# Logits of the first 128 tokens over the first 128 keys alone, in the attention of block 2

## The chip, the core and the metric

The kernel runs on one core of one Trainium2 chip. The core has a matrix engine (TensorE, PE in the profile; its weight loads have a row of their own, PEld), a vector engine (DVE), an activation engine (ACT), a general engine (POOL) and DMA queues, of which SP issues the large loads here. Each engine works through its own list of instructions in order, and semaphores tie the lists together. The metric is the device time of one execution in microseconds (us), lower is better.

## What is computed

The reference chains two transformer blocks on 256 tokens of width 1024. Block 1 (two layers) and its feed-forward are not touched. Block 2 has two layers, each with three kinds of attention over the same 256 tokens, all with heads of 64 channels and all causal:

```python
# moba_attention, 256 tokens are one block: plain causal attention, 6 heads
s_own = jnp.where(kpos_own[None, :] <= t_pos[:, None], s_own, -jnp.inf)
# dsa_attention: 4 index heads rank the keys, the best 64 stay, then 6 heads over one shared key head
idx_score = jnp.where(key_pos[None, :] <= t_pos[:, None], idx_score, -jnp.inf)
_, sel = lax.top_k(idx_score, n_keep)
# dilated_mixture: 3 groups (dilation 1, 4, 16) x 4 slots, a band of keys at or before the token
ok = (dist >= 0) & (dist <= steps) & (blk * C_BLOCK + ki >= C_BLOCK)
```

A token of the first 128 (the first tile, t = 0) can look at keys 0 to 127 at most; a token of the second tile (t = 1) at all 256.

## The kernel before

**Numbers.** Every large product is made of parts in the type fp32r, which TensorE multiplies in one pass: a value is split in a high part and a rest (`whi` and `wlo` for weights, L210 and L211), and `mm3` (L332, its matmuls at L334 to L336) adds three products. Products in plain f32, such as L575 in block 1, the sums over partitions at L355 and the weighing of values at L1003, show two matmul records each in the trace; an fp32r product shows one.

**Logits.** `to_qt` (L430) stacks the high and the low half of one head's queries over the 128 partitions and transposes them (L441), to a tile `qt2` of 128 x 128 for each head and each tile of 128 tokens. `to_kt` (L446) does so for keys (transposes at L458) and writes two planes of 128 x 256 for each head, low over high and high over low. `scores` (L979) then needs two matmuls for one head and one tile of tokens: the query tile is the stationary operand, loaded anew for each, and a plane of 256 keys streams through it, L980 for the first plane and L981 for the second. The result is half of a PSUM bank, `S[:, t * 256:t * 256 + 256]`.

**Who calls it.** In each layer `layer2` (L1119) makes the index logits (L1146, 4 heads and two tiles of tokens), 6 heads with the mask of the selected keys and 6 with the causal mask (`head2`, L1019), and 4 slots of 3 groups (`slot2`, L1032). That is 4 + 12 + 12 = 28 logits of each tile of tokens. Two layers and two matmuls for each make 112 matmuls for the first tile and 112 for the second, 224 in all.

**Who reads it.** `masked_min` (L983, the DVE instruction at L985) adds the mask, scales, and takes the minimum; for t = 0 it reads columns 0 to 127 alone, as does `index_mask` (`S4[h][:, :n]` at L1064). The columns 128 to 255 that the matmuls of the first tile write are read by nobody. Behind it come the exponential (L1010), the scaling (L1013), transposes of the weights (L995, L997), their copy out of PSUM (L999) and the products with the values (L1003).

**Order.** A planner orders each engine's list when the program is built, by priorities (`cur_priority`, the ranks at L274) and by its own estimates of how long instructions take; nothing in the code fixes where between the projections (L334 to L336) a matmul of `scores` lands. PSUM has two banks with the tag `sc` in this part (`att2_banks`, L264).

Of the kernel before, what the change touches and what calls it, by code (L numbers as in the profile page):

```python
# [18 lines left out]
P = 128  # L19
# [223 lines left out]
def ranked(key):  # L243

    def wrap(f):
        def g(self, *a, **k):
            off = self.rank[key]
            self.tc.cur_priority -= off
            r = f(self, *a, **k)
            self.tc.cur_priority += off  # L250
            return r
        return g
    return wrap


class Build:
# [719 lines left out]
        kt = [self.ap.tile([P, 3, 2, 256], F32R, tag="kt2", name="kt2", bufs=self.kt_bufs) for _ in range(0, n, 3)]  # L976
        return [kt[h // 3][:, h % 3] for h in range(n)], kt

    def scores(self, out, q, kt):  # L979
        self.nc.tensor.matmul(out, q, kt[:, 0, :], start=True, stop=False)  # L980
        self.nc.tensor.matmul(out, q, kt[:, 1, :], start=False, stop=True)  # L981

    def masked_min(self, out, S, mask, nm):  # L983

# [33 lines left out]
    @ranked("hd2")  # L1018
    def head2(self, q, kt, masks):  # L1019

        nc = self.nc
        S = self.bank("sc")
        for t in range(2):
            self.scores(S[:, t * 256:t * 256 + 256], q[t], kt)
        p = self.ap.tile([P, 1152], F32, tag="p3", name="p2", bufs=self.p3_bufs)[:, :384]
        nm = self.stat("nm")
        self.masked_min(p[:, :P], S[:, :P], masks[0], nm[:, 0:1])
        self.masked_min(p[:, P:], S[:, 256:512], masks[1], nm[:, 1:2])
        self.softmax2(nm, (p[:, :P], p[:, P:]))
        return p[:, :P], p[:, P:]  # L1030

    def slot2(self, qs, kts):  # L1032

        nc = self.nc
        p = self.ap.tile([P, 1152], F32, tag="p3", name="p3", bufs=self.p3_bufs)
        p0 = p[:, :384].rearrange("p (g k) -> p g k", g=3)
        p1 = p[:, 384:].rearrange("p (g k) -> p g k", g=3)
        nm, n2 = self.stat("nm"), self.stat("n2")
        for t in range(2):
            S = self.bank("sc")  # L1040
            for g in range(2):
                self.scores(S[:, g * 256:g * 256 + 256], qs[g][t], kts[g])
            v = S.rearrange("p (g k) -> p g k", g=2)
            if t == 0:
                self.masked_min(p0[:, 0:2], v[:, :, :P], self.m0[:, 0:2], nm[:, 0:1])
            else:
                self.masked_min(p1[:, 0:2], v, self.m1[:, 0:2], nm[:, 1:2])
        S = self.bank("sc")
        for t in range(2):
            self.scores(S[:, t * 256:t * 256 + 256], qs[2][t], kts[2])  # L1050
        self.masked_min(p0[:, 2], S[:, :P], self.m0[:, 2], n2[:, 0:1])
        self.masked_min(p1[:, 2], S[:, 256:], self.m1[:, 2], n2[:, 1:2])
        nc.vector.tensor_tensor(nm, nm, n2, op=ALU.min)
        self.softmax2(nm, (p[:, :384], p[:, 384:]))
        return [(p0[:, g], p1[:, g]) for g in range(3)]
# [63 lines left out]
    def layer2(self, l, u, rr, rb):  # L1119

        nc, d = self.nc, self.d
        y = [self.half(k, l) for k in range(KT)]
        o_t = lambda: self.ap.tile([P, 256], F32, tag="o2", name="o2", bufs=3)

        ch = self.chunk2(l, 0)
        qi, iws, vb = [], [], []
        kib, ktb = self.new_kt(2)
        for t, ps in enumerate(self.proj_t(ch, u)):
            raw = self.evac2(ps, 452, rr, t)
            vb.append(self.values_of(ps, 384, 1, rr, t))  # L1130
            iw = self.sp.tile([P, 4], F32, tag="iw", name="iw", bufs=2)
            nc.vector.tensor_scalar(iw, raw[:, 448:452], 0.0625, None, op0=ALU.mult)
            iws.append(iw)
            q = self.rope(raw[:, :384], self.rc2[:, t], self.rs2[:, t], 6, "ri")
            dst = self.new_qt()
            self.to_qt(q[:, :256], 4, dst)
            qi.append(dst)
            self.to_kt(q[:, 256:384], 2, ktb, t)
        qb = self.queries(l, 1, u, rr)
        sel = []  # L1140
        for t in range(2):
            S4 = []
            for h in range(0, 4, 2):
                S = self.bank("sc")
                for j in range(2):
                    self.scores(S[:, j * 256:j * 256 + 256], qi[t][:, h + j, :], kib[0])  # L1146
                    S4.append(S[:, j * 256:j * 256 + 256])
            sel.append(self.index_mask(S4, iws[t], t))
        ob = []
        for pr in range(3):  # L1150
            ps = [self.head2([qb[t][:, h, :] for t in range(2)], kib[1], sel) for h in (2 * pr, 2 * pr + 1)]
            pv = self.bank("pv")
            self.weigh(pv, ps, [[vb[t][:, 0, :] for t in range(2)]] * 2, True, True)
            ob.append(o_t())
            nc.scalar.copy(ob[-1], pv[:, :256])

        ka, qa, va = self.keys(l, 2, u, rr), self.queries(l, 3, u, rr), self.values(l, 4, u, rr)
        gates = self.branch_gates(l, 11, u, rb)
        for i in range(3):
            self.gated(ob[i], gates[i], y[3 + i])  # L1160
        cm = (self.m0[:, 0], self.mcausal)
        oa = []
        for pr in range(3):
            hs = (2 * pr, 2 * pr + 1)
            ps = [self.head2([qa[t][:, h, :] for t in range(2)], ka[h], cm) for h in hs]
            pv = self.bank("pv")
            self.weigh(pv, ps, [[va[t][:, h, :] for t in range(2)] for h in hs], True, True)
            oa.append(o_t())
            nc.scalar.copy(oa[-1], pv[:, :256])

        for pr in range(2):
            kc, qc, vc = self.keys(l, 5 + 3 * pr, u, rr), self.queries(l, 6 + 3 * pr, u, rr), self.values(l, 7 + 3 * pr, u, rr)
            if pr == 0:
                gates += self.branch_gates(l, 12, u, rb)
                for i in range(3):
                    self.gated(oa[i], gates[3 + i], y[i])
            ps = [self.slot2([[qc[t][:, 2 * g + i, :] for t in range(2)] for g in range(3)], [kc[2 * g + i] for g in range(3)])
                  for i in range(2)]
            oc = self.bank("pv")
            for g in range(3):  # L1180
                self.weigh(oc, [ps[i][g] for i in range(2)], [[vc[t][:, 2 * g + i, :] for t in range(2)] for i in range(2)],
                           g == 0, g == 2)
            self.gated(oc[:, :256], gates[6 + pr], y[6 + pr])
        return y
# [103 lines left out]
```

## Time and profile before

| | us |
|---|---|
| median of 3 runs | 1556.16 (1555.87 to 1558.52) |
| the profiled execution | 1556.1 |
| its span, first to last instruction | 1554.3 |
| PE busy in the span | 1499.0 |
| DVE busy | 1004.0 |
| ACT busy | 799.3 |
| block 2, attention of layer 1, about 996 to 1180 us | 184 |
| block 2, attention of layer 2, about 1282 to 1465 us | 183 |

How to read it: all rows come from one profiled execution, so sums are made against its 1556.1 us, 1.8 us of which lie outside the span. Matmuls are pipelined, and the length of one record holds its latency too. What a matmul takes from its neighbours is the distance from its start to the start of the next one, called its slot in this document.

### The profile page before, as it was taken

The numbers are of one execution on the slowest core, as the hardware profiler recorded it, in microseconds if no ns is written. First come the engines' busy times: TensorE is split into PE (matmuls) and PEld (weight loads), VectorE is DVE, ScalarE is ACT, GpSimd is POOL, SyncE is SP. The second block draws the span as 40 slices with busy tenths as digits, with TensorE's granted clock in tenths as the row PEclk, the third lists the DMA queues.
The fourth block names the chain that finished last, engine by engine and source line by source line (L and its number), as shares of the span: only waits on it lengthen the run. The fifth ranks groups of instructions, "written<-read, shape, count | busy, mean of one in ns | idle before, by whom it ended". The sixth has DMA issues, their size and how long they took to land.

```text
span 1554.3 us, 25048 instructions
## 1 busy us (share of the span) xinstructions
PE 1499.0 (96%) x9826; PEld 1290.8 (83%) x9826; DVE 1004.0 (65%) x2210; ACT 799.3 (51%) x1498; POOL 70.4 (5%) x83
## 2 busy tenths in 40 slices
PE   5999999999999999999799999999999999999996
PEld 2875688887788789856599999888899999899996
DVE  5675687333333236867565557898767779987675
ACT  3476665321322224567453436677665556876542
POOL 0300000000000000010000000102100010200000
PEclk9999999999999999999999999999999999999998
DMA  9313355333332524362845554434434544334450
GB/s 375 118 55 147 137 193 184 142 109 136 136 109 81 191 80 160 112 221 101 330 148 186 190 182 152 155 124 161 149 132 167 184 146 153 136 114 157 164 188 30
DMA packets 36982, 238.36 MB, mean 153 GB/s; under 512 B 4224, under 2 KB 5888, under 8 KB 15104
## 3 DMA queue, kind: packets, MB, share of 16 engines
q1 hardware_dynamic: 36576, 236.14, 42.8%
q8 instruction: 77, 1.26, 0.3%
q0 software_dynamic: 288, 0.62, 0.2%
q14 instruction: 41, 0.34, 0.1%
HBM read 236.32 MB, written 1.05 MB: 153 GB/s over the span
## 4 chain that ended last, share of the span: by engine, by line
PE 83%; DVE 10%; ACT 3%; DMA 2%; issue 2%; POOL 0%; SPq 0%; DVEq 0%; ACTq 0%; POOLq 0%
PE mm L334 11%; PE mm L335 11%; PE mm L336 11%; PE g L336 6%; PE g L335 6%; PE g L334 6%; PE dn L335 5%; PE dn L336 5%; PE dn L334 5%; DVE wlo L211 3%; PE mm L492 2%; PE tr L635 2%; PE pv L643 2%; DMA raw<-in_w_ada_dram 1%; PE pv L1003 1%
## 5 line engine op out<-in xcount | busy, mean ns | idle before, releaser
L210 ACT CAST whi<-raw 128x1024 fp32r<-128x1024 f32 (+4 forms) x392 | 370.0, 949 | 496.1 <-PE mm L335 137.4
L211 DVE TENSOR_TENSOR wlo<-raw,whi 128x1024 fp32r<-128x1024 f32 (+4 forms) x392 | 431.3, 1105 | 198.1 <-ACT whi L210 196.2
L335 PE MATMUL dn<-Hl,whi 128*128 128x256 f32 (+1 forms) x520 | 161.7, 311 | 0.0
L336 PE MATMUL dn<-Hh,wlo 128*128 128x256 f32 (+1 forms) x520 | 161.0, 310 | 0.4 <-DVE wlo L211 0.4
L334 PE MATMUL dn<-Hh,whi 128*128 128x256 f32 (+1 forms) x520 | 160.6, 310 | 0.0
L334 PE MATMUL mm<-Hh,whi 128*128 128x256 f32 (+1 forms) x512 | 149.3, 292 | 1.0 <-DVE mod L506 0.7
L336 PE MATMUL mm<-Hh,wlo 128*128 128x256 f32 (+1 forms) x512 | 149.9, 293 | 0.0
L335 PE MATMUL mm<-Hl,whi 128*128 128x256 f32 (+1 forms) x512 | 149.3, 292 | 0.0
L334 PE MATMUL mm<-whi,Hh 128*128 128x384 f32 (+2 forms) x352 | 129.1, 367 | 0.0
L336 PE MATMUL mm<-whi,Hl 128*128 128x384 f32 (+2 forms) x352 | 127.3, 362 | 0.0
L335 PE MATMUL mm<-wlo,Hh 128*128 128x384 f32 (+2 forms) x352 | 127.2, 361 | 0.0
L334 PE MATMUL mm<-Fh,whi 128*128 128x256 f32 (+1 forms) x368 | 123.0, 334 | 1.6 <-ACT Fh L539 1.5
L336 PE MATMUL g<-Fh,wlo 128*128 128x256 f32 (+1 forms) x368 | 123.2, 335 | 0.3 <-DVE wlo L211 0.3
L334 PE MATMUL g<-Fh,whi 128*128 128x256 f32 (+1 forms) x368 | 122.6, 333 | 0.0
L335 PE MATMUL g<-Fl,whi 128*128 128x256 f32 (+1 forms) x368 | 122.6, 333 | 0.0
L335 PE MATMUL mm<-Fl,whi 128*128 128x256 f32 (+1 forms) x368 | 122.2, 332 | 0.0
L336 PE MATMUL mm<-Fh,wlo 128*128 128x256 f32 (+1 forms) x368 | 122.1, 332 | 0.0
L335 PEld LDWEIGHTS dn<-Hl,whi 128*128 128x128 f32 x520 | 99.1, 191 | 8.3 <-issue 2.5
L336 PEld LDWEIGHTS dn<-Hh,wlo 128*128 128x128 f32 x520 | 99.1, 191 | 6.3 <-issue 0.8
L334 PEld LDWEIGHTS dn<-Hh,whi 128*128 128x128 f32 x520 | 99.0, 191 | 5.6 <-ACT whi L210 0.5
L334 PEld LDWEIGHTS mm<-Hh,whi 128*128 128x128 f32 x512 | 97.8, 191 | 2.2 <-ACT whi L210 0.8
L336 PEld LDWEIGHTS mm<-Hh,wlo 128*128 128x128 f32 x512 | 97.8, 191 | 1.6 <-issue 0.8
(283 smaller groups left out, 3240.8 us busy)
## 6 DMA issues: line engine op xcount, KB each, us to landing
raw<-in_w_ada_dram SPq DMA_DIRECT2D x48, 1024.0 KB, 4.9
raw<-in_w_gu_dram SPq DMA_DIRECT2D x44, 1024.0 KB, 4.8
raw<-in_w_mix_dram SPq DMA_DIRECT2D x32, 1024.0 KB, 4.8
raw<-in_w_in_dram SPq DMA_DIRECT2D x40, 768.0 KB, 4.3
raw<-in_w_in_dram SPq DMA_DIRECT2D x20, 1024.0 KB, 4.8
raw<-in_w_dn_dram SPq DMA_DIRECT2D x16, 1024.0 KB, 4.8
raw<-in_w_dn_dram SPq DMA_DIRECT2D x12, 768.0 KB, 4.4
raw<-in_w_out_dram SPq DMA_DIRECT2D x8, 1024.0 KB, 4.9
```

The lines of the kernel that those rows point to most:

```text
L210: self.made.append(nc.scalar.copy(hi[:, :m], x))
L211: self.made.append(nc.vector.tensor_tensor(lo[:, :m], x, hi[:, :m].bitcast(F32), op=ALU.subtract))
L334: self.link(nc.tensor.matmul(out, lhs[0], rhs[0], start=start, stop=False))
L335: self.link(nc.tensor.matmul(out, lhs[0], rhs[1], start=False, stop=False))
L336: self.link(nc.tensor.matmul(out, lhs[1], rhs[0], start=False, stop=stop))
L492: made.append(self.nc.tensor.matmul(ps[32 * g:32 * g + 32, :], self.s32[:, 4 * i + g, :], raws[i][:, 512 * g:512 * g + 512], start=i == fi ...
L635: nc.tensor.transpose(ps[:, (2 * j + qt) * P:(2 * j + qt + 1) * P], p[i][:, qt, c:c + P], self.ident)
L643: first(nc.tensor.matmul(pv[i * 64:i * 64 + 64, :256], v, pts[i][0][:, j * 256:j * 256 + 256], start=b == 0 and j == 0, stop=b == nk // 2 ...
L1003: f(nc.tensor.matmul(pv[64 * i:64 * i + 64, c], vs[i][j], pt[:, d], start=first and j == 0, stop=last and j == 1))
```

## The change

`scores` takes a number of columns, and its callers give 128 for the first tile of tokens and 256 for the second. No instruction is added or taken away; 112 of the 224 matmuls stream 128 columns of keys in place of 256 and write 128 columns of PSUM. The stationary operands and their loads stay. No wait is added.

```diff
-    def scores(self, out, q, kt):
-        self.nc.tensor.matmul(out, q, kt[:, 0, :], start=True, stop=False)
-        self.nc.tensor.matmul(out, q, kt[:, 1, :], start=False, stop=True)
+    def scores(self, out, q, kt, n):
+
+        self.nc.tensor.matmul(out, q, kt[:, 0, :n], start=True, stop=False)
+        self.nc.tensor.matmul(out, q, kt[:, 1, :n], start=False, stop=True)
...
         for t in range(2):
-            self.scores(S[:, t * 256:t * 256 + 256], q[t], kt)
+            n = P * (t + 1)
+            self.scores(S[:, t * 256:t * 256 + n], q[t], kt, n)
...
             for g in range(2):
-                self.scores(S[:, g * 256:g * 256 + 256], qs[g][t], kts[g])
+                n = P * (t + 1)
+                self.scores(S[:, g * 256:g * 256 + n], qs[g][t], kts[g], n)
...
         for t in range(2):
-            self.scores(S[:, t * 256:t * 256 + 256], qs[2][t], kts[2])
+            n = P * (t + 1)
+            self.scores(S[:, t * 256:t * 256 + n], qs[2][t], kts[2], n)
...
                 for j in range(2):
-                    self.scores(S[:, j * 256:j * 256 + 256], qi[t][:, h + j, :], kib[0])
+                    n = P * (t + 1)
+                    self.scores(S[:, j * 256:j * 256 + n], qi[t][:, h + j, :], kib[0], n)
```

## Rows read from the trace of the kernel before

**Rows 1.** The page: busy time of each engine, and the granted clock in 40 slices.

```profile
PE 1499.0 (96%) x9826; PEld 1290.8 (83%) x9826; DVE 1004.0 (65%) x2210; ACT 799.3 (51%) x1498; POOL 70.4 (5%) x83
PEclk9999999999999999999999999999999999999998
```

**Rows 2.** Busy time by stretch: block 2's attention of layers 1 and 2.

```profile
core 0: us, PE busy (x) PEld busy (x) DVE busy (x) ACT busy (x) POOL busy (x), PEclk, DMA share, GB/s
996.00:1180.00 184.00, 179.70 (x1294) 166.90 (x1293) 152.62 (x364) 128.03 (x263) 17.02 (x13) 1.00 0.41 142
1282.00:1465.00 183.00, 179.44 (x1292) 166.83 (x1292) 151.74 (x363) 126.11 (x260) 16.23 (x12) 1.00 0.41 143
```

**Rows 3.** Waits by releaser in 996 to 1180 us: PE's longest; DVE's for logits.

```profile
engine line waited for: us in total, times, longest us
PE tq L458 <- DVE ks L452: 1.4, 2, 1.0
PE tq L458 <- DVE kt L463: 1.0, 1, 1.0
PE tr L995 <- DVE p L1013: 0.6, 1, 0.6
...
DVE p L985 <- PE sc L981: 4.3, 9, 0.9
```

**Rows 4.** Lines L980 and L981: durations in ns (min/median/max), first and last start.

```profile
L980 PEld LDWEIGHTS sc<-kt,qt x112: 186/188/192, 997.8 to 1433.6; 128*128 128x128 f32 x112
L980 PE MATMUL sc<-kt,qt x112: 277/282/387, 998.0 to 1433.7; 128*128 128x256 f32 x112
L981 PE MATMUL sc<-kt,qt x112: 277/282/371, 999.6 to 1433.8; 128*128 128x256 f32 x112
```

**Rows 5.** Timeline, a run of logits: start us, length us, engine, line.

```profile
1102.07 0.28 PE L981 MATMUL sc<-kt,qt 128*128 128x256 f32 x1
1102.07 0.19 PEld L980 LDWEIGHTS sc<-kt,qt 128*128 128x128 f32 x1
1102.19 0.28 PE L980 MATMUL sc<-kt,qt 128*128 128x256 f32 x1
...
1102.77 0.28 PE L981 MATMUL sc<-kt,qt 128*128 128x256 f32 x1
```

**Rows 6.** Timeline, projections of 384 columns, nine in a row, first and last.

```profile
1068.20 0.34 PE L336 MATMUL mm<-whi,Hl 128*128 128x384 f32 x1
...
1069.60 0.34 PE L335 MATMUL mm<-wlo,Hh 128*128 128x384 f32 x1
```

**Rows 7.** Timeline, sums over partitions: four matmuls that stream one column.

```profile
1258.69 0.52 PEld L355 LDWEIGHTS tr<-ones,acc 128*128 128x128 f32 x4 [0.31 <-PE mm L336]
1258.72 0.58 PE L355 MATMUL tr<-ones,acc 128*128 128x1 f32 x4
```

**Rows 8.** Timeline, a logits matmul behind a transpose of 128 columns.

```profile
1099.63 0.22 PE L441 MATMUL tq<-ident_r,qs 128*128 128x128 f32 x1
1099.63 0.19 PEld L980 LDWEIGHTS sc<-kt,qt 128*128 128x128 f32 x1
1099.69 0.33 PE L980 MATMUL sc<-kt,qt 128*128 128x256 f32 x1
1099.76 0.14 PEld L441 LDWEIGHTS tq<-ident_r,qs 128*128 128x128 f32 x1
```

**Rows 9.** Transposes of 128 columns in fp32r: a run of four, and line L441.

```profile
1000.41 0.46 PE L441 MATMUL tq<-ident_r,qs 128*128 128x128 f32 x4
...
L441 PEld LDWEIGHTS tq<-ident_r,qs x184: 137/140/146, 90.9 to 1430.8; 128*128 128x128 f32 x184
L441 PE MATMUL tq<-ident_r,qs x184: 221/247/306, 90.9 to 1430.9; 128*128 128x128 f32 x184
```

**Rows 10.** Products in plain f32 in block 1: a run of four records, and line L575.

```profile
702.62 1.88 PE L575 MATMUL sc<-c,raw 128*128 128x512 f32 x4
...
L575 PE MATMUL sc<-c,raw x24: 592/592/697, 67.0 to 703.9; 128*128 128x512 f32 x24
```

**Rows 11.** DVE's reads of the logits, by shape.

```profile
L985 DVE CUSTOM_DVE_ANT_0 p<-sc,mk x56: 269/419/692, 1067.0 to 1434.5; 128x256 f32<-128x256 f32 x28, 128x128 f32<-128x128 f32 x20, 128x512 f32<-128x512 f32 x8
L985 DVE CUSTOM_DVE_ANT_0 p<-sc,sel x24: 268/347/421, 1016.4 to 1328.8; 128x128 f32<-128x128 f32 x12, 128x256 f32<-128x256 f32 x12
```

## The prediction

> **What bounds the kernel now.** I read the page first. PE is busy for 1499.0 of 1554.3 us, no other engine for more than two thirds, and the granted clock stands at its upper level, 2.4 GHz, in nearly every slice [rows 1]. A busy share is a poor witness for matmuls, since the records overlap, so I then asked for the busy time by stretch in the two places that the change touches. In the attention of block 2, PE is without any matmul for 184.00 - 179.70 = 4.30 us in layer 1 and for 183.00 - 179.44 = 3.56 us in layer 2, at a granted clock of 1.00; DVE is next with about 152 us [rows 2]. The waits say what the few idle microseconds are: transposes that wait for DVE, 1.0 us at the most each [rows 3]. So PE issues one matmul behind the other here, in order, and these stages last as long as the sum of its slots. What one slot gains or loses goes to the end nearly whole. What other engines wait for the logits (4.3 us of DVE in layer 1 [rows 3]) is off that path.
>
> The question is therefore only what the slot of a logits matmul is now and what sets it. The record's length, 282 ns [rows 4], does not tell, since it holds the latency. The timeline does: from 1102.07 to 1102.77 there are six slots, so one is 0.70 / 6 = 0.117 us, and the weight load of the next matmul starts at the start of the present one [rows 5].
>
> **What the change does, part by part.** It takes 128 of 256 streamed columns from 112 matmuls: 28 logits of the first tile in a layer, two matmuls each, two layers, which is half of the 224 in the trace [rows 4]. It adds no instruction, no wait and no DMA. The readers are not touched: DVE reads 128 columns where the tokens are those of the first tile already (20 and 12 of its instructions [rows 11]), so neither DVE nor ACT gets less to do. A logit lands at best half a slot earlier, and DVE's wait for it is off the path; I cost that at nothing, covered by PE's own list.
>
> What is left is the slot of an fp32r matmul of 128 columns that loads its own 128 x 128 weights. The trace has no such matmul, so I bound it by the nearest rows.
>
> First, by columns. Eight slots of 384 columns take 1069.60 - 1068.20 = 1.40 us, 0.175 us each [rows 6]. Against 0.117 us for 256, that is 0.058 us for 128 columns, or 0.455 ns a column, with nothing left over as a fixed cost. If columns alone set the slot, the short one takes 0.058 us and the change saves 0.117 - 0.058 = 0.059 us on each, 112 x 0.059 = 6.6 us.
>
> Second, by weight loads. The sums over partitions load weights of 128 x 128 and stream one column. Four of them have records of 0.25 us that end 0.58 us after the first start, so a slot is (0.58 - 0.25) / 3 = 0.11 us with next to nothing to stream; their loads, of 0.19 us, start (0.52 - 0.19) / 3 = 0.11 us apart [rows 7]. Their loads are as long as those of the logits (188 ns [rows 4]), though their type is plain f32. An fp32r case agrees: behind a transpose of 128 columns, the load of a logits matmul starts at 1099.63, and the matmul's record ends at 1099.69 + 0.33 = 1100.02, which with its usual 0.28 means that it streamed from 1099.74. The short transpose did not give its slot to the next matmul: that one came 0.11 us after its load began [rows 8]. So one load takes 0.11 us of the loading path, one load is under way at a time, and a matmul of 256 columns (0.117 us) just covers it. With 128 columns the load is no longer covered, and the slot falls to 0.11 and not to 0.058 us.
>
> Third, upwards. Plain f32 products go slower: four records of 512 columns and 0.592 us end 1.88 us after the first start, (1.88 - 0.592) / 3 = 0.43 us each, 0.84 ns a column, and each product has two such records [rows 10]. At that rate a product of 128 columns would take 2 x 128 x 0.84 ns = 0.215 us.
>
> The ends are thus 0.058 and 0.215 us. I take 0.11, for the rows that share both the load's length and the short stream [rows 7, 8] are nearest. The sum: 112 x (0.117 - 0.110) = 0.8 us, all of it on PE's path. 1556.1 - 0.8 = 1555.3 us for the profiled execution. The median of the runs is 1556.16, 0.1 above the profiled time, so I say 1555.4. About 0.2% (3.1 us) is what a measurement of this kernel can tell from no change, so this is no change.
>
> **The rivals.** A, slower: short fp32r products lose their rate. All fp32r products in the trace that aren't transposes stream 256 columns or more, so no row shows that the single-pass rate of 0.455 ns a column holds below that. If it falls to that of plain f32, each of the 112 slots grows from 0.117 to 0.215 us, and 112 x 0.098 = 11.0 us go to PE's list, of which the idle of 7.9 us in both stages absorbs little, since PE waits there for DVE at other places [rows 3]. That gives 1567.1 us. It decides from a slot of 0.117 + 3.1 / 112 = 0.145 us on. For it: there is no counterexample. Against it: one pass of plain f32 at 128 columns is 0.107 us and would still hide behind the load; only two passes hurt, and an fp32r product shows one record. 22%.
>
> B, faster: the load overlaps better than I think. Fp32r transposes of 128 columns with weights of 128 x 128 do follow each other at (0.46 - 0.22) / 3 = 0.08 us [rows 9]. At that slot the change saves 112 x 0.037 = 4.1 us, 1552.0 us; if columns alone count, 6.6 us, 1549.5 us. Against it: the loads of transposes are shorter, 140 ns against 188 [rows 4, 9]. The Trainium skill ("TensorE: Matmul & The Clock Gate", section "Back-to-back issue gap") gives about 81 ns for 128 columns in a sustained stream, and N/2.4 + 2.5 ns for a gap with no load in it; estimates by these two figures are 1552.1 and 1549.3 us, and this rival would win. The same page (section "LDWEIGHTS") puts a load of 128 columns at P/1.2, 107 ns, and there the trace agrees, with 0.11 us. 8%.
>
> C, the order: the planner places PE's list by estimates that know of the columns, so matmuls of both layers may change places. A group of transposes that comes up before its operand is a new wait of up to 1.0 us, of which layer 1 has two now [rows 3]; four more give 1559.4 us. Fewer of them can give back a part of the 7.9 us idle [rows 2]: half of it, 1551.4 us. 12% for a loss over 3.1 us, 8% for such a gain.
>
> That the change doesn't do what it says (the untouched half of a bank read by somebody) I exclude: the readers' shapes are listed above.
>
> **How the numbers follow.** The forecast has 50%, A 22%, C 12% down and 8% up, B 8%. So faster 0.16, same 0.50, slower 0.34. The likeliest time is 1555.4 us; its own range, with small shifts of the order, is 1553.0 to 1559.0. The range over 8 in 10 has to take in A, as it holds more than 2 in 10 with the outer part of C; with both bounds of the slot it is 1549.5 to 1567.5.
>
> **What would show it.** In the profile of the changed kernel, the two lines of `scores` (L981 and L982 there) should list 56 matmuls of 128 columns and 56 of 256 each, with loads of 188 ns as before. In a run of short logits the starts should be 0.11 us apart (0.06 to 0.08 for B, 0.2 for A), with load and matmul starting in step. PE's busy time is no measure of it: records get shorter by some 0.05 us while slots stay. The two attention stretches should last 184 and 183 us within half a microsecond. New lines in PE's waits, or another sequence of projections and logits, would speak for C. I am wrong if the slot of a short logit is above 0.145 or below 0.089 us, or if stages move by microseconds while slots do not.

## The result, and the profile after

The changed kernel takes 1564.94 us in the median (1564.08 to 1565.91) against 1556.01 us before: a ratio of 1.0051, with a 95% interval from 1.0038 to 1.0063. It is slower by 8.9 us, and the forecast was no change.

The first reading is the one that the prediction asked for, the two lines of `scores` (durations in ns as min/median/max), and the page's busy times.

```profile
PE 1505.1 (96%) x9826; PEld 1291.5 (83%) x9826; DVE 1004.4 (64%) x2210; ACT 799.5 (51%) x1498; POOL 72.3 (5%) x83
...
L981 PEld LDWEIGHTS sc<-kt,qt x112: 186/188/192, 994.7 to 1443.9; 128*128 128x128 f32 x112
L981 PE MATMUL sc<-kt,qt x112: 221/280/387, 994.7 to 1443.9; 128*128 128x128 f32 x56, 128*128 128x256 f32 x56
L982 PE MATMUL sc<-kt,qt x112: 221/278/327, 996.6 to 1444.1; 128*128 128x128 f32 x56, 128*128 128x256 f32 x56
```

The change is there: 56 short and 56 long matmuls on each line, with loads as long as before [rows 4]. The number of instructions on each engine is that of before [rows 1]. Next, a run of short logits in the changed kernel, loads and matmuls in order of time:

```profile
1106.26 0.22 PE L981 MATMUL sc<-kt,qt 128*128 128x128 f32 x1
1106.26 0.19 PEld L982 LDWEIGHTS sc<-kt,qt 128*128 128x128 f32 x1
1106.31 0.28 PE L982 MATMUL sc<-kt,qt 128*128 128x128 f32 x1
1106.37 0.19 PEld L981 LDWEIGHTS sc<-kt,qt 128*128 128x128 f32 x1
1106.43 0.27 PE L981 MATMUL sc<-kt,qt 128*128 128x128 f32 x1
1106.48 0.19 PEld L982 LDWEIGHTS sc<-kt,qt 128*128 128x128 f32 x1
```

The loads start at 1106.26, 1106.37 and 1106.48, 0.11 us apart, where those of 256 columns start 0.117 us apart [rows 5]. A short matmul is not slower than a long one, and hardly faster. So the 8.9 us are somewhere else. Where they are, two marks show: the copy of the row scales at the start of each layer of block 2 (`rr`), and the last scaling of the output (`fin`). First the kernel before, then the changed one; the last two numbers are the first and the last start in us.

```profile
L938 DVE COPY rr<-r x1: 169/169/169, 980.1 to 980.1; 128x2 f32<-128x2 f32 x1
L938 DVE COPY rr<-rr x1: 169/169/169, 1262.4 to 1262.4; 128x2 f32<-128x2 f32 x1
L1258 DVE SCALAR_TENSOR_TENSOR fin<-xs,vec,tr x8: 475/475/480, 1546.2 to 1548.9; 128x256 f32<-128x256 f32 x8
```

```profile
L938 DVE COPY rr<-r x1: 168/168/168, 982.5 to 982.5; 128x2 f32<-128x2 f32 x1
L938 DVE COPY rr<-rr x1: 169/169/169, 1269.2 to 1269.2; 128x2 f32<-128x2 f32 x1
L1263 DVE SCALAR_TENSOR_TENSOR fin<-xs,vec,tr x8: 472/472/479, 1557.3 to 1560.0; 128x256 f32<-128x256 f32 x8
```

From mark to mark, layer 1 of block 2 takes 1262.4 - 980.1 = 282.3 us before and 1269.2 - 982.5 = 286.7 after; layer 2, to the last `fin`, 286.5 before and 290.8 after. That is 4.4 and 4.3 us more. From the first `rr` to the last `fin`, called block 2's own time from here on, it is 568.8 us before and 577.5 after. Block 1, which the change does not touch, moves the first mark about between 980 and 986 us from one profiled execution to the next (2.4 us between these two), so block 2's own time is the sharper measure, and each experiment below is given with it.

Busy time by stretch, from mark to mark of layer 1 (columns as in [rows 2]), the kernel before first:

```profile
980.10:1262.40 282.30, 276.89 (x2048) 262.09 (x2046) 227.42 (x498) 179.98 (x347) 21.23 (x16) 1.00 0.43 150
```

```profile
982.50:1269.20 286.70, 278.56 (x2048) 261.91 (x2046) 227.24 (x499) 180.09 (x347) 23.64 (x16) 1.00 0.43 148
```

With the same 2048 matmuls and the same granted clock, PE is without a matmul for 5.41 us before and for 8.14 after. What it waits for stands in the waits of the matmuls, over block 2 (us in total, times, longest). The kernel before:

```profile
PE tq L458 <- DVE ks L452: 3.6, 6, 1.0
PE tr L367 <- DVE rf L348: 2.5, 1, 2.5
PE tq L441 <- DVE qs L436: 1.7, 3, 0.9
PE tr L355 <- DVE acc L386: 1.5, 1, 1.5
PE tq L458 <- DVE kt L463: 1.3, 2, 1.0
PE tr L995 <- DVE p L1013: 1.2, 2, 0.6
PE sc L980 <- ACT ir L1064: 0.8, 2, 0.4
```

The changed kernel, without the lines that stayed within 0.2 us (`ks`, `rf`, `acc`, `kt` of the transposes) and without two new ones of 0.2 us:

```profile
PE tr L996 <- DVE p L1014: 2.5, 6, 0.7
...
PE tq L441 <- DVE qs L436: 2.3, 4, 0.9
...
PE sc L981 <- ACT ir L1068: 1.5, 2, 0.7
PE sc L981 <- DVE n L986: 1.0, 4, 0.3
PE pv L1004 <- ACT pt L1000: 0.8, 4, 0.2
PE sc L982 <- DVE kt L463: 0.7, 1, 0.7
```

Over all lines the waits come to 12.6 us in 17 places before and to 18.2 us in 33 after. None of the new ones is longer than 0.7 us; there are more of them, at logits, at transposes of the weights and at the products with the values. One of them close up, with the DVE instructions that PE waits for:

```profile
995.15 0.95 DVE L211 TENSOR_TENSOR wlo<-raw,whi 128x768 fp32r<-128x768 f32 x1
...
995.58 0.33 PE L336 MATMUL mm<-whi,Hl 128*128 128x384 f32 x1
996.13 0.42 DVE L463 CAST kt<-tq 64x256 fp32r<-64x256 f32 x1
...
996.60 0.33 PE L982 MATMUL sc<-kt,qt 128*128 128x128 f32 x1 [0.68 <-DVE kt L463]
```

In the new order four projections stand in PE's list between the first plane's logits of the index heads and the second plane's. That plane is finished by a copy on DVE, which stands behind a split of weights of 0.95 us. In the old order the first index logits began at 998.0 us [rows 4], eight projections stood behind them, and the second plane's came at 999.6 us [rows 4] with no such wait. PE works its list in order, so the projections behind that matmul wait too. The planner wrote a different list: in the two traces, leaving aside the width of the logits, 232 of PE's 9826 records stand at another place in the sequence, 96 of DVE's 2210 and 74 of ACT's 1498.

### The profile page after: what moved, and what is told of

It is laid out like the page before. It is cut to its first block, busy times and chain, and to the rows that moved or that the text cites. A ratio compares the mean times of both kernels' runs of the same rounds, so it can differ in the third digit from the quotient of the medians.

```text
span 1564.1 us, 25036 instructions
## 1 busy us (share of the span) xinstructions
PE 1505.1 (96%) x9826; PEld 1291.5 (83%) x9826; DVE 1004.4 (64%) x2210; ACT 799.5 (51%) x1498; POOL 72.3 (5%) x83
## 4 chain that ended last, share of the span: by engine, by line
PE 83%; DVE 10%; ACT 4%; DMA 2%; issue 2%; POOL 0%; SPq 0%; DVEq 0%; ACTq 0%; POOLq 0%
PE mm L334 11%; PE mm L335 10%; PE mm L336 10%; PE g L335 6%; PE g L336 6%; PE g L334 6%; PE dn L335 5%; PE dn L336 5%; PE dn L334 5%; DVE wlo L211 3%; PE mm L492 2%; PE tr L635 2%; PE pv L643 2%; DMA raw<-in_w_ada_dram 1%; PE pv L1004 1%
```

## The experiments

The ratios below are against runs of the kernel before taken beside each experiment (medians of 1558.05 to 1558.23 us), not against the 1556.01 us above.

Two changes are in one here: what a matmul does on the chip, and what the planner makes of it. To part them, a step after planning replaces the access patterns of chosen matmuls and leaves every list, wait and semaphore as it is:

```python
def stream(nc, names, n, w):          # after the planner has placed everything
    ...
                    t = [[1, n]] if n <= w else [[0, n // w], [1, w]]
                    blk.instructions[k] = copy.replace(i, outs=(cut(i.outs[0], [[1, n]]),), ins=(cut(i.ins[0], t), i.ins[1]))
```

**Old order, short matmuls.** The kernel before, with the 112 matmuls narrowed after planning.

```diff
+        if t == 0:
+            FIRST.extend(getattr(i, "ins", i).name for i in made)
...
         program(tc, aps, out)
+    stream(nc, FIRST, 128, 128)
```

> The order of every engine's list is that of the kernel before, instruction by instruction; only the 112 matmuls of the first tile stream 128 columns in place of 256 (narrowed after the planner had placed everything). Theory 1 (the loss of the change sits in the new order; a short logits matmul saves 0.007 us): 0.8 us under the kernel before, some 1555.2 us. Rival (each short matmul itself costs 0.08 us more than a long one): 1565 us, as the changed kernel. Rival (columns set the slot): 6.6 us under before, 1549.4 us.

Measured: 1556.5 us, a ratio of 0.9992 (0.9981 to 1.0004). Its marks:

```profile
L938 DVE COPY rr<-r x1: 168/168/168, 984.8 to 984.8; 128x2 f32<-128x2 f32 x1
...
L1260 DVE SCALAR_TENSOR_TENSOR fin<-xs,vec,tr x8: 475/475/481, 1550.3 to 1553.0; 128x256 f32<-128x256 f32 x8
```

Block 2's own time is 568.2 us, 0.6 less than before. The sum had said 0.8, but three executions in this order, here and below, read 568.8, 568.2 and 568.5 us, so a gain of this size is not shown. Both rivals on the slot are out: neither 11 us more nor 6.6 us less. In the trace PE, DVE and ACT run the same sequence as in the kernel before, and PE's waits, group by group, again come to 12.6 us.

**New order, long matmuls.** The changed kernel, with the same 112 matmuls widened after planning to stream the first 128 keys twice.

```diff
         program(tc, aps, out)
+    stream(nc, FIRST, 256, P)
```

> The order of every engine's list is that of the changed kernel; the 112 matmuls of the first tile stream 256 columns again (the first 128 keys twice, since the other keys may not be there yet in this order), after the planner had placed everything. Theory 1 (order): as slow as the changed kernel or 0.8 us slower, 1565 to 1566 us. Rival (the short matmuls cost): as the kernel before, 1556 us.

Measured: 1566.06 us, a ratio of 1.0052 (1.0036 to 1.0069); block 2's own time is 1559.4 - 981.5 = 577.9 us, 0.4 above the changed kernel's. The sequence of PE, DVE and ACT in the trace is that of the changed kernel. The loss needs no short matmul. These two runs together settle it: the order carries the loss, the columns carry a few tenths of a microsecond at most.

**Shorter still.** Old order; of each pair of the first tile the first matmul streams 128 columns and the second 32.

```diff
+    stream(nc, [f[0] for f in FIRST], 128, 128)
+    stream(nc, [f[1] for f in FIRST], 32, 32)
```

> Order of the kernel before; of each pair of matmuls of the first tile the first streams 128 columns and the second 32. The low-by-high terms stay for 128 keys, the high-by-high ones are left out for keys 32 to 127. Theory (the load of the next weights sets the slot, 0.11 us): no faster than with 128 columns in both, about 1555.2 us. Rival (columns set it): 56 x 96 x 0.455 ns = 2.4 us less than with 128 columns.

Measured: 1557.16 us, a ratio of 0.9994 (0.9982 to 1.0005); block 2's own time 1551.2 - 982.7 = 568.5 us, as with 128 columns in both. The timeline of this kernel, one pair and what follows:

```profile
1104.90 0.22 PE L980 MATMUL sc<-kt,qt 128*128 128x128 f32 x1
1104.90 0.19 PEld L981 LDWEIGHTS sc<-kt,qt 128*128 128x128 f32 x1
1104.96 0.23 PE L981 MATMUL sc<-kt,qt 128*128 128x32 f32 x1
1105.01 0.19 PEld L980 LDWEIGHTS sc<-kt,qt 128*128 128x128 f32 x1
...
1105.12 0.19 PEld L981 LDWEIGHTS sc<-kt,qt 128*128 128x128 f32 x1
```

The loads start 0.11 us apart (1104.90, 1105.01, 1105.12) whether 128 or 32 columns stream in between. The load sets the slot.

**What upset the planner?** The short logits differ for it in two ways: it reckons with fewer columns, and they no longer wait for the second tile's keys. One kernel drops only the wait, and lets the planner see 256 columns:

```diff
+            k = kt[:, p, :n] if n > P else kt[:, p, :n][:, None, :].to_broadcast([P, 2, n])
+            self.nc.tensor.matmul(out, q, k, start=p == 0, stop=p == 1)
```

> The logits of the first tile wait only for the first 128 keys, as in the changed kernel, but stream 256 columns (those keys twice), so the planner reckons with matmuls as long as before; it orders the lists anew. If the planner's order goes wrong because the wait for the other keys is gone: 1560 to 1565 us. If it is because of its estimate of the shorter matmuls: about 1556 us.

The other keeps the wait, and lets it see 128:

```diff
+        k0 = 64 if n == P else 0
+        self.nc.tensor.matmul(out, q, kt[:, 0, k0:k0 + n], start=True, stop=False)
+        self.nc.tensor.matmul(out, q, kt[:, 1, k0:k0 + n], start=False, stop=True)
```

> The planner sees matmuls of 128 columns for the first tile, but they read keys 64 to 191 and so wait for both tiles of keys as before; the logits of the first tile are those of the wrong keys. If the planner's estimate of a shorter matmul upsets the order: slow, 1560 to 1566 us. If the dropped wait did: 1556 us.

Measured: without the wait 1557.14 us, a ratio of 0.9995 (0.9985 to 1.0005), block 2's own time 1550.5 - 981.1 = 569.4 us; with the wait and 128 columns 1564.2 us, 1.0036 (1.0022 to 1.0050), 1559.6 - 983.2 = 576.4 us. So it is the number of columns as the planner sees it that leads to a costly order. In the profiled execution of the kernel that keeps the wait the granted clock also stood at 0.50 for 3.4 us of layer 2 (1321.59 to 1325.01), behind a wait of 2.2 us, which is a part of its 7.6 us. The kernel without the wait has another order as well, 84 of PE's records stand elsewhere in it, and it costs next to nothing.

**Part by part.** The changed kernel with 128 columns in one of its three places only.

```diff
-                    n = P * (t + 1)
+                    n = 256        # in the places that stay long
```

> Only the index heads stream 128 columns (16 of the 112 matmuls). Theory (new waits in PE's list): the trace of the changed kernel has two new waits of 0.7 us at index logits of layer 1, so 2 layers x 1.4 = 2.8 us slower than before, 1559 us. Rival (a cost by the matmul): 16 x 0.08 = 1.3 us.

> Only the 12 plain heads of each layer stream 128 columns (48 of the 112 matmuls). Theory (order): depends on where the planner puts them, between 0 and 6 us slower, 1559 us as the middle. Rival (a cost by the matmul): 48 x 0.08 = 3.8 us, 1560 us.

> Only the mixture's three groups stream 128 columns (48 of the 112 matmuls); PE's list differs from that of before in the fewest places of the three parts (56 against 112 and 144). Theory (order): least of the three, 0 to 2 us slower, 1557 us. Rival (a cost by the matmul): 48 x 0.08 = 3.8 us, 1560 us, as the plain heads alone.

And in two of them:

> Index heads and plain heads stream 128 columns, the mixture 256. Alone the two parts cost 1.3 and 2.4 us of block 2's own time, the mixture 3.8, all three together 8.8. If the parts add up: 3.7 to 5 us of block 2's time, some 572.5 to 573.8 us against 568.8. If the loss lies in how they meet: far from that.

| short in | ratio to before | 95% interval | block 2's own time, us | against before |
|---|---|---|---|---|
| index heads | 1.0000 | 0.9990 to 1.0010 | 570.1 | +1.3 |
| plain heads | 1.0002 | 0.9993 to 1.0012 | 571.2 | +2.4 |
| mixture | 1.0019 | 1.0009 to 1.0028 | 572.6 | +3.8 |
| index and plain heads | 1.0020 | 1.0009 to 1.0030 | 574.6 | +5.8 |
| all three | 1.0051 | 1.0038 to 1.0063 | 577.5 | +8.7 |

My guesses for the parts were poor. The mixture, which I had put least for the fewest moved rows (56 of PE's list), costs most, so how many rows move does not tell what a new order costs; the index heads cost half of what the two waits of 0.7 us had suggested. The differences of 1.3 and 2.4 us are read from one profiled execution each and are below what the timed runs resolve. The last column is measured against one execution of the kernel before, and it comes out 0.8 to 2.7 us above what the ratios say. So whether the index and the plain heads add up (5.8 us together against 1.3 + 2.4) stays open. No cost by the matmul fits either: the plain heads and the mixture have 48 short matmuls each and cost 2.4 and 3.8 us. All five have an order of their own.

**Another estimate, the same work.** As in the first experiment 128 columns on the chip, but planned as 192.

```diff
+        n = 192 if t == 0 else 256
...
+    stream(nc, FIRST, 128, 128)
```

> On the chip the same work as in the kernel with the old order and short matmuls (128 columns in the first tile's logits), but the planner placed them as matmuls of 192 columns. Theory (any other estimate gives another order, and what it costs is not set by the size of the estimate): another order than both kernels, 0 to 9 us slower than before, with PE's waits as the cause. Rival (the loss grows with how much the estimate shrinks): half of the changed kernel's loss, some 1561 us.

Measured: 1577.13 us, a ratio of 1.0114 (1.0097 to 1.0131); block 2's own time 1570.6 - 980.7 = 589.9 us, 21.7 us more than the first experiment, with exactly the same matmuls on the chip. The rival of a loss in step with the estimate falls: a smaller step of the estimate costs more than twice as much. My own theory had 0 to 9 us, and the ratio says some 18. Its waits show what an order can do (us in total, times, longest):

```profile
PE tq L458 <- DVE kt L463: 6.1, 2, 3.0
PE tr L998 <- DVE p L1016: 6.0, 10, 1.4
```

Once in each layer, transposes of keys stand 3.0 us before DVE has done what they wait for, where the longest wait of this kind was 1.0 us before [rows 3]. The granted clock adds to it. Four stretches of the same execution follow, columns as in [rows 2]: the wait in layer 1; the 3.4 us that begin 0.7 us after its end; the time behind them; and a stretch of layer 2, where the clock falls while PE still waits.

```profile
1028.67:1031.70 3.03, 0.00 (x0) 0.00 (x0) 2.97 (x7) 0.00 (x0) 0.39 (x1) 1.00 0.57 231
...
1032.41:1035.82 3.41, 3.41 (x18) 3.41 (x17) 3.34 (x11) 2.07 (x5) 0.00 (x0) 0.50 0.37 67
1035.82:1038.48 2.66, 2.66 (x25) 2.66 (x24) 1.60 (x7) 0.91 (x3) 0.00 (x0) 1.00 0.54 219
1325.95:1332.78 6.83, 6.17 (x30) 6.17 (x31) 6.25 (x20) 2.51 (x5) 0.00 (x0) 0.50 0.34 115
```

At the lower level, 1.2 GHz, the matmuls of 256 columns start 0.213 us apart (1032.62 to 1035.40, 13 slots) in place of 0.12 us. From these slots I estimate that the two falls cost about 4 of the 21.7 us. In the kernel before and in the changed one the clock stays at its upper level through both layers until the last 10 us or so, so no fall of this kind makes up the 8.7 us.

**A remedy by priority.** The changed kernel, with the first tile's logits put lower in the planner's priority (here by 20).

```diff
+        self.tc.cur_priority += 20 if n == P else 0
...
+        self.tc.cur_priority -= 20 if n == P else 0
```

> The changed kernel with the first tile's logits 20 steps lower in the planner's priority, so that short logits come up later behind their operands. Theory (order): if logits that stand too early in PE's list are the loss, part of the 8.8 us comes back, 1558 to 1563 us; if it is no more than another order, anything from 1556 to 1570 us.

> As the kernel before it in this list, 60 steps lower. If logits that come up too early are the loss: 1556 to 1560 us; if the later logits now leave the engines behind PE waiting, slower than with 20 steps.

Measured: 1563.37 us (1.0028, 1.0018 to 1.0038) with 20 steps and 1561.57 us (1.0021, 1.0012 to 1.0031) with 60; block 2's own times are 573.8 and 573.6 us. Some 3.8 of the 8.7 us come back, no more with 60 steps than with 20, and neither reaches the kernel before. Of the kernels that stream 128 columns in all 112 matmuls, only the one of the first experiment is no slower than the kernel before, and its 0.6 us are below what can be timed.

## Why the prediction was wrong

**What bounds the kernel** held: PE's list in order, with its waits, sets the time of these stages. Because it held, a poorer list went to the end nearly whole, 4.4 and 4.3 us in two layers.

**The slot of a short logit** held, value and reason. The sum took 0.110 us against 0.117 and 0.8 us in all; the loads were 0.11 us apart, and block 2 became 0.6 us shorter in the old order, which agrees but is within the scatter. Rival A (the rate of plain f32) and rival B (0.08 or 0.058 us) are both refuted by the same run. The Trainium skill ("TensorE: Matmul & The Clock Gate", section "Back-to-back issue gap") gives about 81 ns for 128 columns in a sustained stream. These fp32r matmuls do not reach it; the measured 0.11 us decides. The same page of the Trainium skill (section "LDWEIGHTS (loading the stationary operand)") puts a load of 128 columns at P/1.2, 107 ns. There the trace agrees, with 0.11 us between loads.

**The step that failed** is the one where the sum was closed: "What is left is the slot". It treated the lists as given and the planner's order as an accident beside the change (rival C, 12% for a loss). But the planner reckons with the columns: each of the ten kernels here that it placed with other operands or priorities had a new list. The cost of that belongs into the sum as a term of unknown sign and size, not among the rivals. The runs put the term at 8.7 + 0.6 = 9.3 us for this order, against at most some 0.6 us of gain from all that the sum had priced. It is the second sign that the prediction had named for being wrong, stages that move by microseconds while slots do not.

**Rival C's price** was mis-sized. Four new waits of 1.0 us gave 1559.4 us. The profile has 33 waits in place of 17, none of the new ones over 0.7 us, and they grew by 18.2 - 12.6 = 5.6 us in both layers together. The other 3 us do not stand in that view, since a gap begins only where the record of the matmul before it ends, and a record is longer than a slot. The wait shown above is an example: from 995.58 to 996.60 is a slot of 1.02 us where projections of 384 columns take 0.175 [rows 6], so it cost 0.85 us and shows as 0.68. Counted in this way in the traces (the slot of the matmul before each gap, short gaps included, less the median slot of its kind), the waits cost 19.5 us in 37 places before and 28.1 us in 56 after, which is 8.6 of the 8.7 us. In the old order with short matmuls it is 19.8 us, in the new order with long ones 26.9 us, 7.4 of its 9.1. How bad an order can be was priced far too low: the kernel planned with 192 columns lost some 18 us by its ratio.

**The dropped wait** on the second tile's keys I had not seen at all. It turned out to cost next to nothing (0.6 us of block 2's own time, within the scatter), so the omission was harmless, but it was luck.

**The range** held 1564.94 us by luck: it reached that far for rival A, for a reason that did not exist.

## What to carry to other kernels

Where a planner writes the order, an edit that changes an operand's size can change the lists of all engines, as it did each time here; its own effect can be measured alone by planning with the old sizes and narrowing afterwards, and a forecast needs a term for the new order as wide as such orders have been seen to differ (here from 0 to some +18 us by the ratios). A matmul that loads its own 128 x 128 fp32r weights gained next to nothing here from fewer than 256 streamed columns (0.117 us), as the load is then the longer of the two (0.11 us). Count what a wait costs from start to start, not by the gap between records. Look at a block's own time between two marks when the rest of the program drifts by more than the effect.

## What I had not expected of the hardware

A wait of PE can cost more than its length: behind the two waits of 3.0 us in the kernel planned with 192 columns the granted clock was 0.50 for 3.4 and 6.8 us, and matmuls of 256 columns started 0.213 us apart in place of 0.12.

The load bounds the slot down to very few columns: with 128 and with 32 streamed columns the loads started 0.11 us apart alike, as in the sums over partitions with one column [rows 7].

Block 2's own time came out within 0.6 us in the kernels that share an order (568.8, 568.2 and 568.5 us; 577.5 and 577.9), while the start of block 2 moves by up to 5.8 us (980.1 to 985.9) between profiled executions of kernels that do the same until then. Much of that can be the clock: it stood at 0.50 for 13.7 us ahead of the earliest start (the kernel before) and for 23.9 us ahead of the latest (20 priority steps). The 10.2 us more at half clock are worth at most 5.1 us, an estimate from these stretches.
